# One shared semaphore for the last three arrivals in front of a final product

## The chip, the cores and the metric

The kernel runs on one core of one Trainium2 chip. The metric is the device time of one execution in microseconds (us), lower is better.

## The reference

For 1024 rows of 4096 float32 each:

```python
loss = np.exp(log_input) - target * log_input
return np.mean(loss, axis=-1).astype(np.float32)
```

The work is to read 33.55 MB once. ScalarE (ACT) makes the exponentials and sums them, VectorE (DVE) makes the products and sums them.

## The kernel before

Each of 128 partitions holds 8 rows. The loads come in one queue (q1 on the page of before), whole rows first; the last row comes in seven pieces, so that little work is left behind the last bytes:

```python
TAIL = [("x", 24), ("t", 12), ("t", 12), ("x", 6), ("t", 5), ("x", 2), ("t", 3)]   # in 32nds of a row
landed = [nc.alloc_semaphore(f"landed{i}") for i in range(len(loads))]             # one per load
```

ACT takes the x pieces (`log_input`), DVE the t pieces (`target`). The partial sums of the last row are written behind the last row's t data, and the x buffer has -1 there. So the last product of DVE (384 elements and 6 partial sums, 390) adds up the whole row as it goes. It needs three things that come late: the last load, the last exponential's sum, and the sum of the product before it. In the kernel before each has its own semaphore:

```python
for j, (lo, w, i) in enumerate(t_work):
    x_load = next(ix for a, wx, ix in x_work if a + wx >= lo + w)
    nc.vector.wait_ge(landed[x_load], 16)
    if j < n_t - 1:
        nc.vector.tensor_tensor_reduce(...).wait_op(landed[i], 16, "sem-ge").then_inc(prod_done, 1)
    else:
        nc.vector.wait_ge(ones_done, 1)
        nc.vector.wait_ge(landed[i], 16)
        nc.vector.wait_ge(prod_done, n_t - 1)
        nc.vector.tensor_tensor_reduce(...     # the last product
        ).wait_op(exp_done, n_x, "sem-ge").then_inc(loss_done, 1)
# (cut) SyncE stores all_loss once loss_done is counted
```

There are two kinds of wait here. `wait_ge` is an instruction in front: the trace of before lists the four of the last product as two of DVE's sequencer (DVEq, `EVENT_SEMAPHORE`, L183 and L184, 50 ns and two conditions each). `wait_op` is a condition on the product itself: the trace lists the exponentials' count with the product (L185), and no instruction for it. `n_x` is 10 exponentials, `n_t` 11 products.

Of the kernel before, what the change touches and what calls it, by code (L numbers as in the profile page):

```python
# [13 lines left out]
def before_first_barrier(nc, instructions):  # L14





    here, first = nc.cur_bb.bb, nc.main_func.blocks[0]  # L20
    names = {i.name for i in instructions}
    here.instructions = [i for i in here.instructions if i.name not in names]
    at = next(
        k
        for k, i in enumerate(first.instructions)
        if i.engine == mybir.EngineType.SP and i.opcode == "Drain"
    )
    first.instructions = first.instructions[:at] + instructions + first.instructions[at:]


def kernel(tc, log_input, target, out):














    nc = tc.nc
    tc.close()
    tc.compile()  # L48

    P = nc.NUM_PARTITIONS  # L50
    n, d = log_input.shape
    nb = n // P
    assert nb * P == n and tuple(target.shape) == (n, d) and nb == 8 and d % 32 == 0
    inv_d = 1.0 / d
    last_row = nb - 1

    x_v = log_input.rearrange("(p b) d -> p (b d)", b=nb)
    t_v = target.rearrange("(p b) d -> p (b d)", b=nb)
    out_v = out.rearrange("(p b) -> p b", b=nb)


    loads = []
    for first, rows in ((0, 4), (4, 2), (6, 1)):
        loads += [("x", first * d, rows * d), ("t", first * d, rows * d)]
    at = {"x": last_row * d, "t": last_row * d}
    for what, w in TAIL:
        loads.append((what, at[what], w * d // 32))
        at[what] += w * d // 32
    assert at == {"x": nb * d, "t": nb * d}


    def work(kind):
        todo = []
        for i, (what, lo, w) in enumerate(loads):
            if what == kind:
                step = min(w, d)
                todo += [(a, step, i) for a in range(lo, lo + w, step)]
        return todo

    x_work, t_work = work("x"), work("t")  # L80
    n_x, n_t = len(x_work), len(t_work)
    n_parts = n_x - last_row + n_t - last_row - 1

    big = {
        "x": nc.alloc_sbuf_tensor("x_big", [P, 4 * d + n_parts], F32).ap(),
        "t": nc.alloc_sbuf_tensor("t_big", [P, 4 * d + n_parts], F32).ap(),
    }
    mid = {
        "x": nc.alloc_sbuf_tensor("x_mid", [P, 2 * d], F32).ap(),
        "t": nc.alloc_sbuf_tensor("t_mid", [P, 2 * d], F32).ap(),  # L90
    }

    def place(what, lo, w):
        row = lo // d
        if 4 <= row < 6:
            return mid[what][:, lo - 4 * d : lo - 4 * d + w]
        if row >= 6:
            lo -= (6 if row == 6 else 4) * d
        return big[what][:, lo : lo + w]

    e_dump = nc.alloc_psum_tensor("e_dump", [P, d], F32).ap()

    parts = nc.alloc_sbuf_tensor("parts", [P, 2 * last_row], F32).ap()
    join_dump = nc.alloc_sbuf_tensor("join_dump", [P, 2 * last_row], F32).ap()
    all_loss = nc.alloc_sbuf_tensor("all_loss", [P, nb], F32).ap()

    def part(k):
        return big["t"][:, 4 * d + k : 4 * d + k + 1]

    landed = [nc.alloc_semaphore(f"landed{i}") for i in range(len(loads))]  # L110
    exp_done = nc.alloc_semaphore("exp_done")
    prod_done = nc.alloc_semaphore("prod_done")
    join_done = nc.alloc_semaphore("join_done")
    ones_done = nc.alloc_semaphore("ones_done")
    loss_done = nc.alloc_semaphore("loss_done")
    out_done = nc.alloc_semaphore("out_done")


    early = []
    for i, (what, lo, w) in enumerate(loads):  # L120
        if what == "x" and lo in (6 * d, 7 * d):
            free = 1 if lo == 6 * d else 4
            nc.sync.wait_ge(exp_done, free)
            nc.sync.wait_ge(prod_done, free)  # L124
        src = x_v if what == "x" else t_v
        dma = nc.sync.dma_start(out=place(what, lo, w), in_=src[:, lo : lo + w])  # L126
        dma.then_inc(landed[i], 16)
        if lo < 6 * d:
            early.append(dma.ins)
    before_first_barrier(nc, early)  # L130


    nc.gpsimd.memset(big["x"][:, 4 * d : 4 * d + n_parts], -1.0).then_inc(ones_done, 1)  # L133


    def join(row, exps):
        nc.scalar.wait_ge(exp_done, exps)
        nc.scalar.activation(  # L138
            out=join_dump[:, 2 * row : 2 * row + 2],
            in_=parts[:, 2 * row : 2 * row + 2],  # L140
            func=ACT_F.Copy,
            scale=inv_d,
            accum_out=all_loss[:, row : row + 1],
        ).wait_op(prod_done, row + 1, "sem-ge").then_inc(join_done, 1)

    for k, (lo, w, i) in enumerate(x_work):
        row, col = lo // d, lo % d
        if col == 0 and row >= 2:
            join(row - 2, k)
        elif col == 0 and row == 1:  # L150
            nc.scalar.wait_ge(exp_done, k)
        nc.scalar.activation(  # L152
            out=e_dump[:, col : col + w],
            in_=place("x", lo, w),
            func=ACT_F.Exp,
            bias=0.0,
            scale=1.0,
            accum_out=parts[:, 2 * row : 2 * row + 1] if row < last_row else part(k - last_row),
        ).wait_op(landed[i], 16, "sem-ge").then_inc(exp_done, 1)
        if col == 0 and row == last_row:  # L160
            join(row - 1, k + 1)


    for j, (lo, w, i) in enumerate(t_work):
        row = lo // d
        x_load = next(ix for a, wx, ix in x_work if a + wx >= lo + w)
        nc.vector.wait_ge(landed[x_load], 16)  # L167
        if j < n_t - 1:
            nc.vector.tensor_tensor_reduce(  # L169
                out=place("t", lo, w),  # L170
                in0=place("t", lo, w),
                in1=place("x", lo, w),
                scale=-1.0,
                scalar=0.0,
                op0=ALU.mult,
                op1=ALU.add,
                accum_out=parts[:, 2 * row + 1 : 2 * row + 2]
                if row < last_row
                else part(n_x - last_row + j - last_row),
            ).wait_op(landed[i], 16, "sem-ge").then_inc(prod_done, 1)  # L180
        else:
            nc.vector.wait_ge(ones_done, 1)
            nc.vector.wait_ge(landed[i], 16)  # L183
            nc.vector.wait_ge(prod_done, n_t - 1)  # L184
            nc.vector.tensor_tensor_reduce(  # L185
                out=place("t", lo, w + n_parts),
                in0=place("t", lo, w + n_parts),
                in1=place("x", lo, w + n_parts),
                scale=-inv_d,
                scalar=0.0,  # L190
                op0=ALU.mult,
                op1=ALU.add,
                accum_out=all_loss[:, last_row : last_row + 1],
            ).wait_op(exp_done, n_x, "sem-ge").then_inc(loss_done, 1)


    nc.sync.wait_ge(join_done, last_row)
    nc.sync.dma_start(out=out_v, in_=all_loss).wait_op(loss_done, 1, "sem-ge").then_inc(
        out_done, 16
    )  # L200
    used = landed + [exp_done, prod_done, join_done, ones_done, loss_done]
    nc.sync.sem_clear(range(used[0].num, out_done.num))
    assert all(used[0].num <= s.num < out_done.num for s in used)
    nc.sync.wait_ge(out_done, 16).then_inc(out_done, -16)
# [30 lines left out]
```

## Time and profile before

| | before |
|---|---|
| time, median of the three runs at hand for the prediction | 84.27 us |
| span of the profiled execution | 82.72 us |
| DMA engines' share of the span with packets | 95.6% |
| DVE busy, ACT busy | 43%, 40% |
| last load landed | 80.410 us |
| from there to the last product's start | 0.261 us |
| from there to the end | 2.311 us |

The times of landings and counts come from the trace's semaphore records: a load is called landed at the sixteenth increment of its semaphore (each of the thirteen has sixteen from DMA), and a product or an exponential is "counted" when its one increment appears. The prediction shows the page's lines and how to read them. What matters is that loads fill all but the end, and the change acts on the last 2.3 us, after the last bytes.

### The profile page before, as it was taken

What the parts mean: (1) busy time and instruction counts of PE and PEld (TensorE: products, weight loads), DVE (VectorE), ACT (ScalarE), POOL (GpSimd) and SP (SyncE); (2) the same over time, 40 slices, a digit from 0 to 9 for tenths busy, and PEclk for the clock granted to TensorE, in tenths of its full rate; (3) what the DMA queues carried; (4) which work ended last, traced back from release to release, by engine and by line L of the source; (5) the groups of instructions that cost most, each with busy time, mean ns of one, the idle gap of its engine ahead of it and who ended that gap; (6) DMA issues with size and microseconds to landing.
All of it is one profiled execution on the core that took longest, in us unless ns stands there. A gap on an engine that the chain in (4) does not pass through costs nothing.

```text
span 82.7 us, 136 instructions
## 1 busy us (share of the span) xinstructions
DVE 35.6 (43%) x22; ACT 33.2 (40%) x35; POOL 0.3 (0%) x5
## 2 busy tenths in 40 slices
DVE  0000000000000000000199999999379995994982
ACT  0500000000499910000000998979792595029360
POOL 0000000000000000000000000000000000000000
DMA  9199999919999991999599699799799999999960
GB/s 507 63 444 507 507 507 507 507 63 444 507 507 507 507 475 63 475 507 507 254 507 475 285 507 507 317 444 507 341 420 404 483 388 436 380 413 428 403 214 2
DMA packets 2016, 33.56 MB, mean 406 GB/s; under 512 B 352, under 2 KB 608, under 8 KB 1120
## 3 DMA queue, kind: packets, MB, share of 16 engines
q1 hardware_dynamic: 2016, 33.56, 95.6%
HBM read 33.55 MB, written 0.00 MB: 406 GB/s over the span
## 4 chain that ended last, share of the span: by engine, by line
DMA 72%; DVE 14%; issue 10%; SPq 2%; DVEq 0%
DMA t_big<-in_target_dram 72%; DVE t_big L169 13%; SPq L126 2%; DVE t_big L185 1%; DVE parts L169 0%; DVEq L184 0%; DVEq L183 0%; DVEq L167 0%; SPq L124 0%; DVE all_loss L185 0%
## 5 line engine op out<-in xcount | busy, mean ns | idle before, releaser
L169 DVE CUSTOM_DVE_ANT_0 t_big<-t_big,x_big 128x4096 f32<-128x4096 f32 (+2 forms) x8 | 26.2, 3308 | 43.4 <-DMA t_big<-in_target_dram 43.2
L152 ACT ACTIVATE e_dump<-x_big 128x4096 f32<-128x4096 f32 (+3 forms) x8 | 21.8, 2730 | 23.9 <-DMA x_big<-in_log_input_dram 23.6
L138 ACT ACTIVATE join_dump<-parts 128x2 f32<-128x2 f32 x7 | 1.4, 203 | 20.4 <-DVE parts L169 20.3
L169 DVE CUSTOM_DVE_ANT_0 t_mid<-t_mid,x_mid 128x4096 f32<-128x4096 f32 x2 | 8.8, 4422 | 2.0 <-DMA t_mid<-in_target_dram 2.0
L152 ACT ACTIVATE e_dump<-x_mid 128x4096 f32<-128x4096 f32 x2 | 7.1, 3568 | 0.0
L152 ACT ACT_TABLE_LOAD x1 | 1.3, 1283 | 3.0 <-PEq L48 3.0
L152 ACT ACTIVATION_READ_ACCUMULATOR e_dump<-x_big 128x1 f32 x8 | 1.5, 186 | 0.0
L138 ACT ACTIVATION_READ_ACCUMULATOR join_dump<-parts 128x1 f32 x7 | 1.3, 187 | 0.0
L185 DVE CUSTOM_DVE_ANT_0 t_big<-t_big,x_big 128x390 f32<-128x390 f32 x1 | 0.6, 568 | 0.2 <-ACT e_dump L152 0.2
L169 DVE DVE_READ_ACCUMULATOR2_ANT parts<- 128x1 f32 x7 | 0.6, 83 | 0.0
L152 ACT ACTIVATION_READ_ACCUMULATOR e_dump<-x_mid 128x1 f32 x2 | 0.4, 186 | 0.0
L169 DVE DVE_READ_ACCUMULATOR2_ANT t_big<- 128x1 f32 x3 | 0.3, 84 | 0.0
L133 POOL MEMSET x_big<- 128x6 f32 x1 | 0.1, 103 | 2.5 <-POOLq L48 2.5
L219 POOL MEMSET const-uint8-127<- 128x1 uint8 x1 | 0.1, 102 | 0.0
L219 POOL MEMSET const-bfloat16-1.0<- 128x1 bf16 x1 | 0.1, 101 | 0.0
L219 POOL MEMSET const-float32-0.0<- 128x1 f32 x1 | 0.1, 98 | 0.2 <-issue 0.2
L219 POOL MEMSET const-float32-1.0<- 128x1 f32 x1 | 0.1, 98 | 0.0
L185 DVE DVE_READ_ACCUMULATOR2_ANT all_loss<- 128x1 f32 x1 | 0.1, 85 | 0.0
## 6 DMA issues: line engine op xcount, KB each, us to landing
x_mid<-in_log_input_dram SPq DMA_DIRECT2D x1, 4096.0 KB, 49.9
t_mid<-in_target_dram SPq DMA_DIRECT2D x1, 4096.0 KB, 59.1
x_big<-in_log_input_dram SPq DMA_DIRECT2D x1, 2048.0 KB, 19.8
t_big<-in_target_dram SPq DMA_DIRECT2D x1, 2048.0 KB, 24.3
x_big<-in_log_input_dram SPq DMA_DIRECT2D x1, 1536.0 KB, 15.3
t_big<-in_target_dram SPq DMA_DIRECT2D x2, 768.0 KB, 17.5
x_big<-in_log_input_dram SPq DMA_DIRECT2D x1, 384.0 KB, 18.7
t_big<-in_target_dram SPq DMA_DIRECT2D x1, 320.0 KB, 19.1
```

The source lines that it names most:

```text
L126: dma = nc.sync.dma_start(out=place(what, lo, w), in_=src[:, lo : lo + w])
L133: nc.gpsimd.memset(big["x"][:, 4 * d : 4 * d + n_parts], -1.0).then_inc(ones_done, 1)
L138: nc.scalar.activation(out=join_dump[:, 2 * row : 2 * row + 2], in_=parts[:, 2 * row : 2 * row + 2], func=ACT_F.Copy, scale=inv_d, accum_o ...
L152: nc.scalar.activation(out=e_dump[:, col : col + w], in_=place("x", lo, w), func=ACT_F.Exp, bias=0.0, scale=1.0, accum_out=parts[:, 2 * ro ...
L169: nc.vector.tensor_tensor_reduce(out=place("t", lo, w), in0=place("t", lo, w), in1=place("x", lo, w), scale=-1.0, scalar=0.0, op0=ALU.mult ...
L185: nc.vector.tensor_tensor_reduce(out=place("t", lo, w + n_parts), in0=place("t", lo, w + n_parts), in1=place("x", lo, w + n_parts), scale= ...
L219: nc = _bacc.Bacc("TRN2", target_bir_lowering=False, num_devices=1)
```

## The change

The intent is to take the sequencer's waits for late arrivals out from between the last arrival and the last product. The last load (16 increments), the product before (1) and the last exponential (1) all count on `last_ready`, and the last product itself waits for 18. Conditions on older events stay with the sequencer. Beside that, five of ten waits on x loads go, where the wait before was for a load issued later. The thirteen loads landed in the order of their issue (before: from 21.709 to 80.410).

```diff
-    landed = [nc.alloc_semaphore(f"landed{i}") for i in range(len(loads))]
+    landed = [nc.alloc_semaphore(f"landed{i}") for i in range(len(loads) - 1)]
+    last_ready = nc.alloc_semaphore("last_ready")
...
-        dma.then_inc(landed[i], 16)
+        dma.then_inc(landed[i] if i < len(loads) - 1 else last_ready, 16)
...
-        ).wait_op(landed[i], 16, "sem-ge").then_inc(exp_done, 1)
+        ).wait_op(landed[i], 16, "sem-ge").then_inc(
+            exp_done if k < n_x - 1 else last_ready, 1
+        )
...
-        nc.vector.wait_ge(landed[x_load], 16)
+        if j == 0 or x_load > t_work[j - 1][2]:
+            nc.vector.wait_ge(landed[x_load], 16)
...
-            ).wait_op(landed[i], 16, "sem-ge").then_inc(prod_done, 1)
+            ).wait_op(landed[i], 16, "sem-ge").then_inc(
+                prod_done if j < n_t - 2 else last_ready, 1
+            )
...
-            nc.vector.wait_ge(landed[i], 16)
-            nc.vector.wait_ge(prod_done, n_t - 1)
+            nc.vector.wait_ge(exp_done, n_x - 1)
+            nc.vector.wait_ge(prod_done, n_t - 2)
...
-            ).wait_op(exp_done, n_x, "sem-ge").then_inc(loss_done, 1)
+            ).wait_op(last_ready, 18, "sem-ge").then_inc(loss_done, 1)
```

More of the change, by code (lines that the diff above doesn't have):

```diff
@@ L200 @@
     )
-    used = landed + [exp_done, prod_done, join_done, ones_done, loss_done]
+    used = landed + [last_ready, exp_done, prod_done, join_done, ones_done, loss_done]
     nc.sync.sem_clear(range(used[0].num, out_done.num))
```

## The prediction

> **What bounds the kernel now.** I read first the page's busy tenths, its queue part and its chain by line, to see what kind of kernel this is.
>
> ```profile
> DVE  0000000000000000000199999999379995994982
> ACT  0500000000499910000000998979792595029360
> DMA  9199999919999991999599699799799999999960
> q1 hardware_dynamic: 2016, 33.56, 95.6%
> DMA t_big<-in_target_dram 72%; DVE t_big L169 13%; SPq L126 2%; DVE t_big L185 1%; DVE parts L169 0%; DVEq L184 0%; DVEq L183 0%; DVEq L167 0%; SPq L124 0%; DVE all_loss L185 0%
> ```
>
> The reader is to see that one queue of loads is at work from the first slice to the last but one, that VectorE (DVE) and ScalarE (ACT) are busy 43% and 40%, and that the chain is loads for 72% of the span. 33.55 MB have come in by 80.41 us, which is 417 GB/s; nothing in the change touches that. What it can touch is the short part after the last bytes, so the second view is the chain in order of time from the last loads on.
>
> ```profile
> 60.46 19.11 DMA t_big<-in_target_dram
> 79.57 0.02 issue
> 79.60 0.83 DVE t_big L169 x2
> 80.43 0.01 issue
> 80.44 0.05 DVEq L183
> 80.49 0.05 issue
> 80.54 0.05 DVEq L184
> 80.59 0.09 issue
> 80.67 0.57 DVE t_big L185
> 81.24 0.01 DVE all_loss L185
> ```
>
> Columns: start in us, length in us, what. DVEq is VectorE's sequencer. Between the end of the product before (80.43) and the start of the last product (80.67) there is no work in the chain, only two semaphore instructions of 0.05 us and the gaps around them: 0.24 us. The timeline of the same stretch shows the other arms that the last product needs, and what follows it.
>
> ```profile
> 79.60 0.83 DVE L169 CUSTOM_DVE_ANT_0 t_big<-t_big,x_big 128x640 f32<-128x640 f32 x1
> 79.95 0.39 ACT L152 ACTIVATE e_dump<-x_big 128x256 f32<-128x256 f32 x1 [0.27 <-DMA x_big<-in_log_input_dram]
> 80.28 0.19 ACT L152 ACTIVATION_READ_ACCUMULATOR e_dump<-x_big 128x1 f32 x1
> 80.35 0.08 DVE L169 DVE_READ_ACCUMULATOR2_ANT t_big<- 128x1 f32 x1
> 80.67 0.57 DVE L185 CUSTOM_DVE_ANT_0 t_big<-t_big,x_big 128x390 f32<-128x390 f32 x1 [0.24 <-ACT e_dump L152]
> 81.27 0.35 SPq L198 DMA_DIRECT2D out_dram<-all_loss  x1
> ```
>
> The bracket blames the exponential, but that ended at 80.28 + 0.19 = 80.47, and the product began 0.20 later. So the exponential isn't what held it to the end. The semaphore records of the trace settle it, in us from the span's start: the last load's sixteenth increment at 80.410, the product before it counted at 80.441, the last exponential at 80.471. The last one is 0.200 before 80.671. The sequencer saw the last load 0.028 after it landed (80.438), began its second wait 0.098 later (80.536), and the product began 0.135 after that: 0.261 us from landing to start, in a row, while the two other arms came in.
>
> [...] the four explicit waits of the last product have become two such instructions of two conditions each (lines 183 and 184), and one condition, the exponentials' count, is on the product itself. [...] products released by a load from their own wait start 0.023 to 0.024 after the sixteenth increment (41.050 to 41.074, 75.847 to 75.871, 79.572 to 79.596), and ScalarE's joins 0.022 to 0.023 after a product's count (45.520 to 45.542). [...] the sequencer's next semaphore instruction came 0.015 to 0.016 after the start of a held product, 41.090 after 41.074 and 75.886 after 75.871, though its own condition was long true. [...] here a two-condition wait lasts 0.050 and the next starts 0.098 after it. [...]
>
> **The change part by part.**
> 1. The last load, the last exponential and the product before count on one semaphore, and the last product waits for 18 in its own wait. What stays in front of it are four conditions again, hence two semaphore instructions, but on older events: the last part of log_input landed at 79.930, the exponential before at 79.694, the product two before at 79.545, the fill with -1 at 3.1. The earliest that the sequencer gets to them is 79.61, after the product before has started. Then it waits for the 79.930: 79.958 by the same 0.028, second wait 80.056 by the same 0.098, and the product [...] could start at 80.191 by the same 0.135. That is 0.280 before the last of its three arms, so the two waits lie wholly beside the load and the exponential.
> 2. The product then starts at the latest of 80.410, 80.441 and 80.471, plus 0.023: 80.494 in place of 80.671. Gain: 0.177 us, all on the path that sets the end.
> 3. Behind the product nothing changes: 0.586 from its start to its count (81.257), 0.017 to the store's issue (81.274), 1.413 to the store's last increment (82.687), 0.034 to the end (82.721).
> 4. Five of the products' waits on a load of log_input go: for the 2nd to 4th, 6th and 9th product, where the target load waited for just before was issued later.
>
> ```profile
> L167 DVEq EVENT_SEMAPHORE  x10: 21/21/21, 21.7 to 78.8; - x10
> ```
>
> They cost 5 x 0.021 = 0.105 us of the sequencer, at 41.09, 41.28, 41.47, 60.52 and 75.89, each time while a product of 1.76 or 4.42 us runs. The next product starts either 4.345 to 4.351 after its forerunner, with no idle time, or when its load lands (77.743 to 77.766). Gain: 0.
> 5. One semaphore fewer for loads and one more for the common count: the same range to clear, after the store is issued. Gain: 0.
> Sum: 0.18 us. 84.27 - 0.18 = 84.09 us; the span of 82.72 would be 82.54. In parts of the whole: 0.2%.
>
> **The rivals.**
> *The whole wait goes.* If the load were always last, the gain would be 0.261 - 0.024 = 0.237, 84.03 us. For it: the load is the arm with the longest tail behind it now. Against: exponential and product land 0.061 and 0.031 after it in this execution; with loads closer together or further apart that moves, so the gain may lie between some 0.12 and 0.24.
> *The wait is only moved.* A product held [...] might be released late, or the sequencer might not run its waits while the product before is at work. Then they would come at 80.44 as now, and nothing or less than nothing is gained: 84.27, or 84.4. For it: the sequencer was seen not to pass a held product. Against: it did run its waits (41.09, 41.28, 41.47) 0.02 to 0.4 into a running product of 4.4 us, and the product before the last starts at 79.596, 0.9 before the time that counts.
> *The gain is lost behind.* An earlier store might land later for the memory's own reasons. The page gives that term as one sample.
>
> ```profile
> out_dram<-all_loss SPq DMA_DIRECT2D x1, 4.0 KB, 1.4
> ```
>
> No load competes with it by then, so I expect it unchanged. The result would be between 84.09 and 84.27.
> *The removed early waits speed the products*, so that loads waiting for free buffers go out earlier. Against: those issues wait for the first and fourth product (58.56), whose starts are 4.35 apart with no gap, and the queue's share is 95.6%. It would give no more than hundredths.
>
> **Range and chances.** The gain of 0.18 is about as large as the spread of the times before (84.16 to 84.43, from the fastest to the slowest 0.27), so the range is mostly that spread: a median of some runs may lie 0.1 off on either side in both kernels, and the gain itself 0.06. I choose 84.09 with 83.90 to 84.30. A change of 2% is 1.7 us; the whole stretch from the last landing to the end is 2.31 us, of which the store takes 1.41. Nothing in the change can give or take that; I leave 0.005 on each side for what I don't see.
>
> **What would show it right or wrong.** Right: the gap between the end of the product before and the start of the last product falls from 0.24 us to some 0.06; the chain no longer holds DVEq at lines 183 and 184 but the exponential or the product before, with the product some 0.023 after the last of the three counts; the sequencer's two waits before the last product lie near 79.96 and 80.06; five waits in place of ten at the products' line; 0.586, 0.017, 1.41 behind unchanged. Wrong: semaphore instructions still after 80.4, a product that starts over 0.05 after the eighteenth count, a start-to-start time of the early products other than 4.35, or a loads' end that moves by more than a tenth.

The forecast's sum is the 0.177 us of step 2, rounded to 0.18, and zero from steps 3 to 5, so 84.27 - 0.18 = 84.09 us. That it is safe to wait for 18 on a semaphore with three kinds of writers was the assumption then; the five experiments that do so gave correct results.

## The result

The median is 84.09 us (83.97 to 84.23, 6 runs), against 84.19 us (84.14 to 84.43, 6 runs) for the kernel before in the same comparison. The ratio is 0.9983, with a 95% interval of 0.9967 to 1.0. A ratio here is made from the runs of the two kernels, so it isn't quite the ratio of the medians. By the 2% line the two are the same; whether the small gain is real, and whose it is, the trace and the experiments tell.

First the chain of waits of the changed kernel, in order of time (start, length, what), its last pieces but the one after the last product:

```profile
61.30 18.97 DMA x_big<-in_log_input_dram
80.28 0.02 issue
80.30 0.52 ACT e_dump L155 x2
80.82 0.02 issue
80.84 0.57 DVE t_big L193
```

No DVEq piece is left. The chain runs from a load of `log_input` through the last exponential straight into the last product, with 0.02 us between them. Six lines of the timeline of the same stretch have the arms (the three late arrivals that the last product needs) and the store:

```profile
79.95 0.83 DVE L175 CUSTOM_DVE_ANT_0 t_big<-t_big,x_big 128x640 f32<-128x640 f32 x1
80.30 0.39 ACT L155 ACTIVATE e_dump<-x_big 128x256 f32<-128x256 f32 x1 [0.23 <-DMA x_big<-in_log_input_dram]
80.62 0.19 ACT L155 ACTIVATION_READ_ACCUMULATOR e_dump<-x_big 128x1 f32 x1
80.70 0.08 DVE L175 DVE_READ_ACCUMULATOR2_ANT t_big<- 128x1 f32 x1
80.84 0.57 DVE L193 CUSTOM_DVE_ANT_0 t_big<-t_big,x_big 128x390 f32<-128x390 f32 x1
81.44 0.35 SPq L206 DMA_DIRECT2D out_dram<-all_loss  x1
```

The product before ends at 80.79 and the last product starts at 80.84, a gap of 0.05 where it was 0.24. Its bracket with a releaser is gone. The semaphore records say the same to the nanosecond: last load 80.745, product 80.798, exponential 80.818, start 80.841, which is 0.023 after the eighteenth count.

The waits that remain, by their lines (duration in ns: least, median, most; first and last start in us), each from the view of one source line:

```profile
L173 DVEq EVENT_SEMAPHORE  x5: 21/21/21, 22.1 to 79.1; - x5
...
L191 DVEq EVENT_SEMAPHORE  x1: 50/50/50, 80.1 to 80.1; - x1
...
L192 DVEq EVENT_SEMAPHORE  x1: 111/111/111, 80.2 to 80.2; - x1
```

Ten waits at the products' line have become five. The two in front of the last product are done by 80.311, half a microsecond before its start. The 111 ns of the second are not its cost: it began at 80.200 and was held by its second condition, the last `log_input` load, until that landed at 80.277.

This profiled execution is itself longer than that of before (span 82.88 us against 82.72). The trace shows why. Its very first load landed at 22.076 us in place of 21.709, and this lateness of 0.37 us is still 0.335 us at the last load. That first load is issued at the very start of the span by an instruction that the change leaves alone. It was the slowest of its six (84.23 us). So the two spans must not be compared; the part after the last landing can be. It takes 2.139 us in place of 2.311, which is 0.172 us less.

### The profile page after: what moved, and what is told of

Same layout as the page of the kernel before. It is cut to its first block, busy times and chain, and to the rows that moved or that the text cites. A ratio compares the mean times of both kernels' runs of the same rounds, so it can differ in the third digit from the quotient of the medians.

```text
span 82.9 us, 131 instructions
## 1 busy us (share of the span) xinstructions
DVE 35.6 (43%) x22; ACT 33.2 (40%) x35; POOL 0.3 (0%) x5
## 3 DMA queue, kind: packets, MB, share of 16 engines
q1 hardware_dynamic: 2016, 33.56, 95.5%
HBM read 33.55 MB, written 0.00 MB: 405 GB/s over the span
## 4 chain that ended last, share of the span: by engine, by line
DMA 72%; DVE 18%; issue 4%; SPq 3%; ACT 1%
DMA t_big<-in_target_dram 49%; DMA x_big<-in_log_input_dram 23%; DVE t_big L175 17%; SPq L129 3%; DVE t_big L193 1%; ACT e_dump L155 1%; DVE parts L175 0%; SPq L127 0%; DVE all_loss L193 0%
```

## The experiments

My theory: what counts is where the last product waits. A condition left to the sequencer is paid for after its event: in the profile of before its wait is an instruction that starts 0.027 to 0.028 us after the event (65.379 to 65.406, 80.410 to 80.438), and the last product starts 0.135 after the start of the last such wait (80.536 to 80.671). A condition on the product itself costs only the 0.023 us (0.023 to 0.024 after a landing there). Written as a rule for this kernel, the start is the later of (the last event that the sequencer waits for + 0.162 us) and (the last event that the product waits for + 0.023 us). Where both sequencer waits come after the load, another 0.096 to 0.098 is added (80.438 to 80.536 in before). Rivals: the five removed waits made the gain; the exponential alone sets the start, as the idle row of before names it; or the gain was chance.

All twelve runs gave correct results. They ran in batches on three chips (4, 12 and 14 in the record), each ratio against the kernel before in the same batch. Times in the tables below are us; "tail" is from the last landing to the end of the span in the profiled execution.

**The changed kernel again** (no edit).

> The changed kernel once more, as the yardstick of this chip. My theory: a last product that starts 0.023 us after the last of its three arms (load, product before, exponential), 0.06 to 0.11 us after the last load has landed; 0.14 to 0.20 us faster than before, a ratio of 0.9977 to 0.9984. Rival (the gain of the first comparison was chance): a ratio of 1.000 within 0.001.

Measured: 83.96 against 84.19 (9 runs of before), ratio 0.9973, interval 0.9960 to 0.9986. The product started 0.024 after the last arm and 0.100 after the last landing; tail 2.146. The gain isn't chance; its centre here is a little above what I expected.

**The common semaphore alone**, all ten waits kept.

```diff
-        if j == 0 or x_load > t_work[j - 1][2]:
-            nc.vector.wait_ge(landed[x_load], 16)
+        nc.vector.wait_ge(landed[x_load], 16)
```

> The common semaphore with all ten earlier waits put back. My theory: these run while a product is at work, so the time is that of the changed kernel within 0.05 us (ratio to before 0.9977 to 0.9985) and the early products still start 4.345 to 4.351 us apart. Rival (the removed waits made the gain): the time of the kernel before, ratio 1.000, with early products further apart.

Measured: 84.02 (five runs, 83.91 to 84.30), ratio 0.9977 (0.9963 to 0.9992), tail 2.132. The early products started 4.350, 4.346 and 4.346 apart, as in the kernel before (4.351, 4.346, 4.345).

**The five waits taken out alone**, semaphores as before.

```diff
-        nc.vector.wait_ge(landed[x_load], 16)
+        if j == 0 or x_load > t_work[j - 1][2]:
+            nc.vector.wait_ge(landed[x_load], 16)
```

> The kernel before without the five waits, and nothing else. My theory: no gain, ratio 0.9995 to 1.0005; the last product still starts 0.26 us after the last load has landed, behind two sequencer waits. Rival (the removed waits made the gain): ratio 0.998.

Measured: 84.19 against 84.19, ratio 0.9998 (0.9985 to 1.0012), tail 2.310. The chain of waits of this kernel has the same two sequencer pieces as before:

```profile
80.59 0.02 DVEq L184
80.61 0.05 issue
80.66 0.05 DVEq L185
80.71 0.08 issue
80.79 0.57 DVE t_big L186
```

The whole gain belongs to the common semaphore, none to the removed waits.

**One sequencer wait fewer in the kernel before.**

```diff
+    nc.vector.wait_ge(ones_done, 1)
     for j, (lo, w, i) in enumerate(t_work):
...
-        nc.vector.wait_ge(landed[x_load], 16)
+        if j < n_t - 1:
+            nc.vector.wait_ge(landed[x_load], 16)
...
-            nc.vector.wait_ge(ones_done, 1)
```

> The kernel before, with the wait for the fill moved to the start and the last product's wait on its log_input load left to its own later load, so that two conditions are left for the sequencer (last load, product before) and one semaphore instruction should do in place of two. My theory: the start is 0.027 to 0.028 us after the later of the two, plus 0.135: with a load and a product 0.03 to 0.05 us apart that is 0.19 to 0.22 us after the last landing in place of 0.26, a gain of some 0.07 us. Rival (the exponential alone sets the start, as the idle row names it): no change in the start.

Measured in one look: one semaphore instruction with two conditions is left. It began at 80.623, 0.028 after the later of load and product (80.595), and the last product started 0.134 later, at 80.757. That is 0.189 after the last landing, and the tail is 2.232, 0.079 less than before. The exponential was counted at 80.645, so it did not set this start. The single time, 84.14, can't tell 0.08 us.

**Eight useless waits in front of the last product**, in the kernel before and in the changed one; twenty-four in the changed one. They wait on loads that landed long ago.

```diff
+            for i_old in range(8):      # 24 in the third kernel
+                nc.vector.wait_ge(landed[i_old % 6], 16)
             nc.vector.tensor_tensor_reduce(   # the last product
```

> The kernel before with eight more waits on long landed loads in front of the last product, four more semaphore instructions. My theory: in the kernel before the sequencer's waits lie on the path, 0.098 us each, so the last product starts 0.39 us later, 0.65 us after the last landing: some 84.58 us, ratio 1.0047. Rival (the sequencer's waits run beside the arms, and the exponential sets the start): less than 0.20 us.

> The same eight waits in the changed kernel. My theory: the sequencer is ready 0.42 us before the last arm there, and the 0.39 us fit into it: no more than 0.03 us over the changed kernel, ratio to before 0.998 to 0.9985, product still 0.023 us after the eighteenth count. Rival (sequencer waits cost the same wherever they stand): 0.39 us more than the changed kernel, ratio 1.003.

> Twenty-four such waits in the changed kernel, twelve semaphore instructions, 1.18 us. My theory: some 0.44 us of it are hidden and the rest is on the path: 0.73 us over the changed kernel, ratio to before 1.0065 to 1.0075. Rival (the waits are dropped or free once the product waits on itself): no change; rival (all counted): 1.18 us, ratio 1.012.

| | median | ratio to before (95%) | tail |
|---|---|---|---|
| before + 8 | 84.40 | 1.0026 (1.0011 to 1.0041) | 2.482 |
| changed + 8 | 84.13 | 0.9990 (0.9974 to 1.0005) | 2.143 |
| changed + 24 | 84.52 | 1.0035 (1.0019 to 1.0052) | 2.673 |

The directions came as expected; two sizes did not. In the kernel before I expected 0.39 us and the tail grew by 0.171 (by time 0.22). The chain shows where I miscounted:

```profile
80.62 0.05 DVEq L186
80.67 0.05 issue
80.72 0.05 DVEq L186
80.77 0.05 issue
80.81 0.05 DVEq L186
80.86 0.09 issue
80.95 0.57 DVE t_big L187
```

The twelve conditions were paired anew. Two of the six instructions had no late condition and came first, at 79.706 and 79.802. The third, from 79.899 on, held the product's count, and ended 0.035 after it (80.536 to 80.571). Three came behind it, 0.098 apart, and then 0.134 to the start. So two instructions more than before lie behind the first late condition, not four.

In the changed kernel eight such waits cost nothing in the trace: the last of six instructions began at 80.264, the product started at 80.675, still 0.024 after the last count, and the tail is that of the changed kernel. The timed ratio is above the range that I gave; its interval reaches down into it, so the times alone would not have shown that the waits are free. In the chain they are absent:

```profile
80.13 0.52 ACT e_dump L155 x2
80.65 0.02 issue
80.67 0.57 DVE t_big L195
```

With twenty-four, fourteen instructions from 80.049 to 81.319 ran at 0.098 each, and the product started 0.134 after the last of them: 0.545 after the last count. The overflow is 0.52 us (0.545 - 0.023), not 0.73. I had let them start only when the last `log_input` load had landed (80.368 in that execution), but that condition was paired into the last instruction, so nothing blocked the thirteen before.

**One of the three arms left to the sequencer.** Three kernels, each with two arms on the common semaphore and one apart.

```diff
 # product apart
-                prod_done if j < n_t - 2 else last_ready, 1
+                prod_done, 1
-            nc.vector.wait_ge(prod_done, n_t - 2)
+            nc.vector.wait_ge(prod_done, n_t - 1)
-            ).wait_op(last_ready, 18, "sem-ge")
+            ).wait_op(last_ready, 17, "sem-ge")
 # exponential apart
-            exp_done if k < n_x - 1 else last_ready, 1
+            exp_done, 1
-            nc.vector.wait_ge(exp_done, n_x - 1)
             nc.vector.wait_ge(prod_done, n_t - 2)
+            nc.vector.wait_ge(exp_done, n_x)
-            ).wait_op(last_ready, 18, "sem-ge")
+            ).wait_op(last_ready, 17, "sem-ge")
 # load apart
-        dma.then_inc(landed[i] if i < len(loads) - 1 else last_ready, 16)
+        dma.then_inc(landed[i], 16)
+            nc.vector.wait_ge(landed[i], 16)
-            ).wait_op(last_ready, 18, "sem-ge")
+            ).wait_op(last_ready, 2, "sem-ge")
```

> Only the last load and the last exponential share the semaphore (17); the product before is waited for by the sequencer, on its own semaphore. My theory: start 0.027 + 0.135 = 0.162 us after the product before is counted, so with arms as in the profile of before 0.11 us later than in the changed kernel. Rival (sharing two of three gives the whole gain, as only the last arm counts): start 0.023 us after the last exponential.

> Only the last load and the product before share the semaphore (17); the exponential is waited for by the sequencer. My theory: start 0.162 us after the exponential is counted, some 0.14 us later than in the changed kernel. Rival: as the changed kernel within 0.03 us.

> Only the product before and the last exponential share the semaphore (2); the last load is waited for by the sequencer. There are five conditions in front, three semaphore instructions, of which the one with the load should come last with one condition alone (0.021 us in place of 0.050). My theory: start 0.13 to 0.16 us after the last landing, some 0.05 to 0.08 us later than in the changed kernel. Rival (the exponential alone counts): 0.023 us after the last exponential.

| apart | load | product | exponential | start | start minus the arm apart | start minus last arm | tail |
|---|---|---|---|---|---|---|---|
| product | 80.622 | 80.670 | 80.705 | 80.832 | 0.162 | 0.127 | 2.254 |
| exponential | 80.681 | 80.704 | 80.740 | 80.900 | 0.160 | 0.160 | 2.269 |
| load | 80.711 | 80.780 | 80.816 | 80.872 | 0.161 | 0.056 | 2.202 |
| none (changed, again) | 80.575 | 80.610 | 80.651 | 80.675 | | 0.024 | 2.146 |

The start follows the arm that the sequencer waits for by 0.160 to 0.162 us, whichever it is, even when another arm on the product's own wait came later. In all three that arm was the first condition of its instruction. Where the late one was the second, the instruction ended 0.034 to 0.035 after it (80.277 to 80.311 in the changed kernel, 80.536 to 80.571 in that of before with eight waits), against 0.077 here (80.670 to 80.747); so 0.162 holds for the first place alone. The chain of the kernel with the product apart ends like this:

```profile
80.58 0.10 DVE t_big L175
80.67 0.03 issue
80.70 0.05 DVEq L192
80.75 0.09 issue
80.83 0.57 DVE t_big L193
```

Sharing two of three therefore gives a part of the gain only: the tails lie between 2.146 and 2.311. For the load, my guess that its instruction would have one condition was wrong (it was paired with the last `log_input` load), and its start came at the upper end of the range given. The times (84.22, 84.29, 84.26, before 84.25) are too coarse for this; the trace decides.

**Both kernels once more.** By then the profiles had the last landing at 80.41 to 80.57 us in the four kernels with three semaphores and at 80.58 to 80.82 in the eight with a shared one, which looked like a cost of sharing.

> The kernel before, unchanged, as a null test, for its profile too: in the four profiles with three separate semaphores so far the last load landed at 80.41 to 80.57 us, in the eight with a shared one at 80.58 to 80.82. My theory (which execution falls to the profiler decides): ratio 1.000 within 0.0015, and a last landing that may lie anywhere from 80.4 to 80.8; from the last landing to the end 2.31 us. Rival (the shared semaphore delays the loads): a last landing under 80.58.

> The changed kernel a third time. My theory: 2.14 us from the last landing to the end, 0.17 less than before, a ratio of 0.9973 to 0.9985, and a last landing that may lie anywhere from 80.4 to 80.8. Rival (the shared semaphore delays the loads by some 0.19 us, which eats the gain): a last landing over 80.58, and a ratio of 1.000.

Measured: the kernel before had its last landing at 81.006, later than any other, the changed one at 80.452, nearly the earliest. So neither group holds, and I take the grouping for chance among the executions that fall to the profiler: a delay of 0.19 us would have eaten the timed gain, which it did not. The null test gave a ratio of 1.000 (0.9978 to 1.0022), tail 2.300; the changed kernel 83.97 against 84.21, ratio 0.9971 (0.9952 to 0.9991), tail 2.142, product 0.023 after the last count.

## Why the prediction was right

- **The bound.** Loads still fill the span (95.5% of it with packets) and nothing in the change moved them. Their end wanders by 0.6 us between executions of the two kernels as they are (80.41 to 81.01), more than three times the gain. I had named a loads' end that moves by more than a tenth as a sign of error; it moved by 0.335 in the first profile. The sign was badly chosen: repeats showed it in both directions in unchanged code.
- **Step 1, the waits move beside the arms.** They did, but the working had the pairs wrong. The first instruction waited for the exponential before the last (counted 80.075) and the fill, the second for the last `log_input` load (80.277), and its end came 0.034 after that. With the 0.084 from such an end to a start (0.134 less the 0.050 of a two-condition wait) the product could have started at 80.395. That leaves 0.423 to the last count at 80.818, against 0.280 predicted. More slack, same result. So the sign "near 79.96 and 80.06" did not come true: in the profile whose last landing is nearest to that of before (80.452), the two waits began some 0.19 earlier, at 79.773 and 79.871.
- **Step 2, the gain.** 0.177 us predicted. The tails are 2.311 and 2.300 in the two profiles of the kernel before, 2.139, 2.146 and 2.142 in the three of the changed one: 0.154 to 0.172 us. It is a little less than predicted because the exponential came 0.073 to 0.076 after the load in these, not 0.061. The release of 0.023 on a product's own wait was found again for a count of 18 raised by a load, DVE itself and, last, ACT: 0.023, 0.024, 0.023 in the three profiles.
- **Step 3, behind the product.** 0.585 from start to count in place of 0.586, and 1.458 from there to the end in place of 1.464. Unchanged.
- **Steps 4 and 5.** Zero predicted. The removed waits measured 0.9998 by themselves. The clearing of the semaphores takes 0.062 us in the first profile of either kernel and is over 0.9 us before the end, beside the store.
- **The time.** 84.09 predicted and measured in the first comparison. That agreement to the hundredth is luck: the changed kernel's three medians are 84.09, 83.96 and 83.97, with ratios 0.9983, 0.9973 and 0.9971. Their mean, 0.9976, is 0.20 us of 84.2; the trace's 0.16 (a ratio of 0.9981) lies within each interval.
- **The rivals.** Of the count of 18, seventeen increments come from others than DVE (sixteen of the load, one of ACT). The load as the last arm did not occur in any of the three profiles of the changed kernel: product and exponential came 0.035 to 0.053 and 0.073 to 0.076 after it. The wait that is only moved, the gain lost behind and the early waits are ruled out above, by the start 0.023 after the last count, by the equal times behind it, and by the two runs that part the changes.

I found no version that beats both. What is left in the tail by the changed kernel is 0.10 from landing to start, 0.585 of product, and 1.46 of store. The tail's sizes leave little: an element moved from the t piece before the last into the last one lets the last `log_input` piece land earlier by its 512 bytes at 417 GB/s, 1.2 ns, but makes the last product longer by (0.826 - 0.568) us / 250 elements = 1.0 ns. With 0.073 to 0.077 us between the start and the earliest that the load allows, that is some 60 elements and 0.01 us. This is an estimate from the durations and the loads' mean rate (33.55 MB by 80.41 us in before), and I ran no kernel of it.

## What to carry to other kernels

When one instruction needs several late arrivals, put those that arrive last on its own wait, if need be by letting them count on one semaphore that takes nothing else, and leave only old events to the sequencer: here the product started 0.023 to 0.024 us after the last count on its own wait, and 0.160 to 0.162 after an arm left to the sequencer as the first condition of its instruction. In these runs waits by the sequencer cost nothing while they were done in time (eight more: product still 0.024 after the last count), and were paid in full beyond that (twenty-four more: 0.52 us); so look at when the waits happen, not at how many there are. A gain of a few tenths of a microsecond is read from the stretch of the trace that it acts on, since the loads' end wandered by more here (0.6 us, 80.41 to 81.01).

## What the traces show of the waits

- A wait by DVE's sequencer with one condition took 0.021 us (L167 of before), one with two conditions that were already true 0.050 (L183, L184). From one such two-condition wait to the next it was 0.096 to 0.098, and 0.133 to 0.135 from the start of the last one to the start of the product.
- Conditions were paired in another order than the program's: in the kernel before, the program has the last `log_input` load, the fill, the last load, the product before; the trace has the last load with the fill (L183), then the product with the `log_input` load (L184). This misled me four times (step 1 of the prediction, and the expectations for before + 8, changed + 24 and the load apart). A late condition that fell into an early pair held all pairs behind it (80.536 to 80.948 in the kernel before with eight more waits).
- An instruction's own wait was released 0.022 to 0.024 us after the last count in the profiles of before and after, be it a load's (products and exponentials), a product's (ACT's joins) or an exponential's (the last product of after). Where a product was held by its own wait, the sequencer's next semaphore instruction came only after that product had started (41.090 after 41.074, 60.517 after 60.502, 75.886 after 75.871), so in this kernel the sequencer did not run on past a held product, though it ran three waits (41.090, 41.281, 41.472) beside a running one.
- Sharing one load's semaphore with two single counts and waiting for their full sum of 18 was correct in the five experiments that do it, and shortened the tail by 0.15 to 0.17 us in the changed kernel.
